# Transpositions of x and B in the chunk stage in the rounded 32-bit type

## The chip, the cores and the metric

The kernel runs on one core of a Trainium2 chip. The core has five engines that work side by side: TensorE (PE in the profile; its weight loads have a row of their own, PEld), VectorE (DVE), ScalarE (ACT), GpSimd (POOL) and SyncE (SP), which here only starts transfers. The metric is device microseconds of one execution; lower is better. Three runs of the kernel before took 1293.86, 1295.33 and 1298.93 us; the median is 1295.33.

## The reference, cut to what matters

One layer of a decoder: a prompt of 1024 rows and 64 sample rows go through a norm, a large projection, two branches (a pooling branch and a state-space branch, "SSD") and a gated sum. The change lies in the state-space branch of the prompt. There the rows are cut into 8 chunks of 128, and the 32 heads stand in 4 groups of 8. For each group and chunk the reference does this:

```python
def step(h, inp):
    xq, dq, Bq, Cq = inp
    acs = jnp.cumsum(dq * Ag, axis=1)
    seg = acs[:, :, None] - acs[:, None, :]
    decay = jnp.exp(jnp.where(mask, seg, -jnp.inf))
    cb = jnp.einsum('bign,bjgn->bijg', Cq, Bq)
    att = cb[..., None] * decay * dq[:, None]
    y = jnp.einsum('bijge,bjgep->bigep', att, xq)
    y = y + jnp.einsum('bign,bige,bgepn->bigep', Cq, jnp.exp(acs), h)
    last = acs[:, -1]
    w_in = jnp.exp(last[:, None] - acs) * dq
    h = h * jnp.exp(last)[..., None, None] + jnp.einsum('bjgn,bjge,bjgep->bgepn', Bq, w_in, xq)
    return h, y
```

`xq` is a chunk of x (512 channels for a group), `Bq` and `Cq` its 128 state columns, and `h` the state that goes from chunk to chunk.

## The kernel before, in words

**Number types.** TensorE takes 32-bit data in two declared types: plain (F32 in the code) and rounded (F32R). For accuracy, the large products are split: a matrix is cut into a rounded part and a rounded rest ("hi" and "lo"), and three products of the rounded type (hi x hi, hi x lo, lo x hi) stand for one. Smaller products are made in the plain type; each of these appears as two pairs of a weight load and a matmul. A transposition is made on TensorE too: the data are loaded as weights and an identity matrix is streamed through, so that the transposed data land in PSUM. There is one identity, `ident`, in the plain type (L112), and all transpositions are in that type. Each is one weight load and one matmul.

**Stages by time.** Up to about 120 us the inputs are normed and transposed and the first products run; the order on every engine is written out by hand there. From 120 to 832 us the projection runs, in Strassen's manner, with convolutions, pooling and the sample part of the state-space branch beside it. From 832 to 1122 us is the chunk stage, which the change touches. Then come the last output products, up to 1297 us.

**The chunk stage.** `chunk(g, c)` (L1382) is a generator for group g and chunk c; there are 4 x 8 = 32. The convolved x, B and C were stored channels-first in DRAM. A chunk loads them as `xb` (six blocks of 128x128: four of x, then B, then C), loads the running sums of the decays into `dec`, copied to all 128 partitions, has ScalarE make `cE` and the eight exponentials of `dec` (L1196) and POOL put in the mask (L1187). Then come the lines that the change touches: four transpositions of x into one PSUM bank `px` (L1400), one of B into another bank `pbc` (L1402), and, in the plain type, the product of B and C beside it (L1403). ScalarE copies the transposed B to a rounded part `bt` (L1406), VectorE makes `xd` from `px` (L1412) and scales `px` in place (L1413); ScalarE and VectorE split it into `xw` and `xwl` (L1415, L1419), and B's rest is `btl` (L1420). VectorE multiplies the decays with the product of B and C (L1416) and `cE` with C (L1418). Next, `inner` (L1203) makes the chunk's output with small plain products (L1208, L1211), three split products make the state's update (L1429 to L1431), and `finish` (L1360) gates and splits the output.

**What sets the order.** The instructions of a chunk are woven with large output products (`products`, L1682, which runs blocks of `gemm_`, L348, with its three split products L354 to L356). TensorE's order in this stage is that of the program text: `in_line` ties each of its instructions to the one before. ScalarE, VectorE, POOL and SyncE are ordered by a planner, which at build time goes through the program with modelled costs and puts on each engine what is ready, by priority; `behind` pins a few pieces. Buffers matter too: `xd`, `bt`, `btl`, `xw` and `xwl` have one buffer each, `dec`, `xb` and `sz` three.

Of the kernel before, what the change touches and what calls it, by code (L numbers as in the profile page):

```python
# [9 lines left out]
F32R = mybir.dt.float32r  # L10
# [10 lines left out]
P = 128  # L21
# [25 lines left out]
def tile_pool_ssd_step(  # L47
# [6 lines left out]
    nc = tc.nc  # L54
    uid = [0]

    def nm(s):
        uid[0] += 1
        return f"{s}_{uid[0]}"
# [33 lines left out]
    def Y4(pool, dt=F32R):  # L93
        return pool.tile([P, 4, T], dt, tag="Y", name=nm("Y"), bufs=2)

    def PB():
        return psB.tile([P, 512], F32, tag="ps", name=nm("ps"))
# [4 lines left out]
    def const(shape, name, dt=F32):  # L102
        return cp.tile(shape, dt, tag=name, name=name)
# [7 lines left out]

    ident = const([P, P], "ident")  # L112
    make_identity(nc, ident)
    blk = const([NS, NB], "blk")
    nc.gpsimd.memset(blk, 1.0)
    nc.gpsimd.affine_select(blk, blk, [[-8, NB]], ALU.is_ge, 0.0, base=0, channel_multiplier=1)
# [1062 lines left out]
    def decays(dec, g, c):  # L1179

        S = P if c < NC else NS
        load(dec, acs_d[c, 8 * g:8 * g + 8, :S].partition_broadcast(S))

    def far(dec, c):

        if c < NC:
            nc.gpsimd.affine_select(dec, dec, [[0, 8], [1, P]], ALU.is_ge, FAR, base=0, channel_multiplier=-1)  # L1187
        else:
            dS = dec.rearrange("p h (b i) -> p h b i", i=8)
            nc.gpsimd.affine_select(dS, dS, [[0, 8], [8, NB], [1, 8]], ALU.is_ge, FAR, base=0, channel_multiplier=-1)  # L1190
            nc.gpsimd.affine_select(dS, dS, [[0, 8], [-8, NB], [0, 8]], ALU.is_ge, FAR, base=0, channel_multiplier=1)

    def exps(dec, g, c):
        S = P if c < NC else NS
        for h in range(8):
            act(dec[:, h], dec[:, h], AF.Exp, bias=acT[:S, c, 8 * g + h:8 * g + h + 1], scale=-1.0)  # L1196
# [6 lines left out]
    def inner(xd, dec, S, state=None, cE=None):  # L1203
        pi = PB()
        for q in range(4):
            o = [pi[64 * hh:64 * hh + 64, q * S:(q + 1) * S] for hh in range(2)]
            for hh in range(2):
                mm(o[hh], xd[:S, 2 * q + hh, :], dec[:S, 2 * q + hh], start=True, stop=state is None)  # L1208
            for hh in range(2 if state is not None else 0):
                h = 2 * q + hh  # L1210
                mm(o[hh], state[:, h * 64:h * 64 + 64], cE[:, h], start=False, stop=True)  # L1211
        return pi[:, :4 * S].rearrange("p (q i) -> p q i", i=S)
# [144 lines left out]
    def ckt(shape, tag, bufs=2):  # L1357
        return (cl if tag in CKL else ca if tag in ("dec", "xb", "cE") else ck).tile(list(shape), F32, tag=tag, name=nm(tag), bufs=bufs)

    def finish(g, o, S, v, sz):  # L1360

        V.tensor_tensor(v, v, sz, ALU.mult)
        act(sz, v, AF.Square)
        nc.gpsimd.tensor_tensor(sz[:, 0:2], sz[:, 0:2], sz[:, 2:4], ALU.add)
        sa = sq_acc[:, o:o + S]
        if g == 0:
            nc.gpsimd.tensor_tensor(sa, sz[:, 0], sz[:, 1], ALU.add)
        else:
            nc.gpsimd.tensor_tensor(sz[:, 0], sz[:, 0], sz[:, 1], ALU.add)
            nc.gpsimd.tensor_tensor(sa, sa, sz[:, 0], ALU.add)  # L1370
        yhc = yh[g][:, :, o:o + S]
        act(yhc, v, AF.Copy)
        nc.gpsimd.tensor_tensor(yl[g][:, :, o:o + S], v, yhc.bitcast(F32), ALU.subtract)
# [8 lines left out]
    def chunk(g, c):  # L1382
        o = c * P
        xb = ckt([P, 6, P], "xb", 3)
        load(xb, xbc_d[g][:, :, o:o + P])
        Bf, Cf = xb[:, 4], xb[:, 5]
        dec = ckt([P, 8, P], "dec", 3)
        decays(dec, g, c)
        yield
        if c > 0:  # L1390
            cE = ckt([P, 8, P], "cE")
            act(cE, dec, AF.Exp, scale=-1.0)
        far(dec, c)
        exps(dec, g, c)
        yield
        sz = ckt([P, 4, P], "sz", 3)
        load(sz, z_d[g][:, :, o:o + P])
        px = PB()
        for q in range(4):
            nc.tensor.transpose(px[:, q * P:(q + 1) * P], xb[:, q], ident)  # L1400
        pbc = PB()
        nc.tensor.transpose(pbc[:, :P], Bf, ident)  # L1402
        mm(pbc[:, P:2 * P], Bf, Cf, start=True, stop=True)  # L1403

        bth, btl = (ck.tile([P, P], F32R, tag=t, name=nm(t), bufs=1) for t in ("bt", "btl"))
        act(bth, pbc[:, :P], AF.Copy)  # L1406
        if c > 0:
            act(pbc[:, 2 * P:3 * P], Cf, AF.Copy)
        pxv = px.rearrange("p (h d) -> p h d", d=64)
        heads = slice(8 * g, 8 * g + 8)  # L1410
        xd = ckt([P, 8, 64], "xd", 1)
        V.tensor_tensor(xd, pxv, dtT[:, c, heads].unsqueeze(2).to_broadcast([P, 8, 64]), ALU.mult)  # L1412
        V.tensor_tensor(pxv, pxv, wdT[:, c, heads].unsqueeze(2).to_broadcast([P, 8, 64]), ALU.mult)  # L1413
        xwh, xwl = (ck.tile([P, 512], F32R, tag=t, name=nm(t), bufs=1) for t in ("xw", "xwl"))
        act(xwh, px, AF.Copy)  # L1415
        V.tensor_tensor(dec, dec, pbc[:, P:2 * P].unsqueeze(1).to_broadcast([P, 8, P]), ALU.mult)  # L1416
        if c > 0:
            V.tensor_tensor(cE, cE, pbc[:, 2 * P:3 * P].unsqueeze(1).to_broadcast([P, 8, P]), ALU.mult)  # L1418
        V.tensor_tensor(xwl, px, xwh.bitcast(F32), ALU.subtract)  # L1419
        V.tensor_tensor(btl, pbc[:, :P], bth.bitcast(F32), ALU.subtract)  # L1420
        xD = ckt([P, 4, P], "xD")
        for q in range(4):
            act(xD[:, q], xb[:, q], AF.Copy, scale=Dv[:, 4 * g + q:4 * g + q + 1])
        yield
        if c == 0:
            yh[g], yl[g] = [Y4(hs if g % 2 else hp) for _ in range(2)]
        pi = inner(xd, dec, P, *((hst[g], cE) if c > 0 else ()))
        pu = PB()
        mm(pu, bth, xwh, start=True, stop=False)  # L1429
        mm(pu, btl, xwh, start=False, stop=False)  # L1430
        mm(pu, bth, xwl, start=False, stop=True)  # L1431
        hn = ckt([P, 512], "hst", 2)
        if c == 0:
            V.tensor_copy(hn, pu)
        else:
            nc.gpsimd.tensor_tensor(hn.rearrange("p (h d) -> p h d", d=64), hst[g].rearrange("p (h d) -> p h d", d=64),
                                    Elb[:, c, heads].unsqueeze(2).to_broadcast([P, 8, 64]), ALU.mult)
            V.tensor_tensor(hn, hn, pu, ALU.add)
        hst[g] = hn

        v = ckt([P, 4, P], "v")
        V.tensor_tensor(v, pi, xD, ALU.add)
        finish(g, o, P, v, sz)
        if c == NC - 1:
            yield
            pt = PB()
            for q in range(4):
                nc.tensor.transpose(pt[:, q * P:(q + 1) * P], hn[:, q * P:(q + 1) * P], ident)
            fo = ckt([P, 4, P], "xD")
            act(fo, pt.rearrange("p (q n) -> p q n", n=P), AF.Copy)  # L1450
            store_(new_ssm_p[0, 0, 8 * g:8 * g + 8].rearrange("(q h) p n -> (h p) q n", h=2), fo)
# [127 lines left out]
    def to_chunks():  # L1579
        nonlocal right, ca  # L1580
        right.__exit__(None, None, None)
        right = tc.tile_pool(name="ca", bufs=3, side="right", reuse_waits="tile")
        ca = right.__enter__()
        right_all.append(right)
        seq.extend(chunk(g, c) for g in range(NG) for c in range(NC))
        next(seq[0])
# [288 lines left out]
    for i in range(8):  # L1875
# [7 lines left out]
        if last_:  # L1883
            q, s3 = hs.tile([P, T], F32, tag="sq", name="q", bufs=1)[:, :D], const([P, 4], "s3")
        rl = sso[:, i:i + 1]
        out = y_prompt[0, i * P:(i + 1) * P, :]
# [59 lines left out]
```

## Time and profile before

| what | value |
|---|---|
| median of three runs | 1295.33 us |
| span of the profiled execution | 1297.1 us |
| its own time | not given beside the span; the span stands for it |
| TensorE busy | 1255.9 us, 97% |
| weight loads busy | 1173.9 us, 90% |
| VectorE / ScalarE / POOL busy | 70% / 55% / 52% |
| chunk stage, 832 to 1122 us | TensorE busy 280.9 of 290 us |

In the lines of the profile, L1400 is line 1400 of the kernel; `ps<-ident,xb` says that the tile `ps` is written from `ident` and `xb`, the moving operand first and then the weights. `128*128 128x128` is the size of the weights and then of the moving operand. A list of a line's instructions gives the shortest, median and longest duration in ns; the timeline gives start and length in us; a row of the waits gives who waited for whom, the sum in us, the number of waits and the longest. Matmuls overlap, and the ends of their records are modelled: what one costs in a row of them is the step from start to start. Both number types stand as `f32` where the shape of a matmul is given.

### The profile page before, as it was taken

To read this page: it belongs to the slowest core of one execution; us is meant where nothing else is said; L and a number is where in the kernel's file an instruction comes from. 1 tells how busy PE (TensorE), PEld (TensorE's weight loads), DVE (VectorE), ACT (ScalarE), POOL (GpSimd) and SP (SyncE) were. 2 spreads that over 40 slices of the span, in tenths; PEclk is the share of its full clock that TensorE was granted. 3 is DMA by queue.
4 is the path that set the end of the run, shared out by engine and by line. 5 is a ranking of instruction groups with operands and counts; after the bars stand their busy time and mean duration, and the time that the engine had idled before them with its cause. 6 is when DMAs were issued, how large, how long until landed. Compare 5 with 4: busy or idle time off the path is not lost.

```text
span 1297.1 us, 26554 instructions
## 1 busy us (share of the span) xinstructions
PE 1255.9 (97%) x9771; PEld 1173.9 (90%) x9771; DVE 910.5 (70%) x1580; ACT 708.8 (55%) x1684; POOL 677.4 (52%) x563
## 2 busy tenths in 40 slices
PE   7999999999999999999999999999998999999998
PEld 6779999989999999999889999889998999999786
DVE  4685778866979578775777665488676888576433
ACT  4665356375656564545455453687987868201111
POOL 1007668677869776664344444276776747314000
PEclk9999999999999999999999999999999999999999
DMA  9837345465455544444656555999988656575631
GB/s 326 259 107 224 119 150 173 142 202 170 146 180 197 165 155 133 161 135 129 181 158 173 152 178 164 356 355 354 338 270 262 202 168 199 172 266 159 226 106 52
DMA packets 233795, 251.70 MB, mean 194 GB/s; under 512 B 31265, under 2 KB 177905, under 8 KB 233658
## 3 DMA queue, kind: packets, MB, share of 16 engines
q1 hardware_dynamic: 161568, 171.60, 42.1%
q10 hardware_dynamic: 72098, 78.41, 17.5%
q8 instruction: 77, 1.26, 0.4%
q14 instruction: 52, 0.43, 0.1%
HBM read 167.06 MB, written 83.01 MB: 193 GB/s over the span
## 4 chain that ended last, share of the span: by engine, by line
PE 67%; issue 8%; DMA 8%; DVE 6%; POOL 5%; ACT 4%; SPq 0%; ACTq 0%; POOLq 0%; DVEq 0%
PE ps L603 6%; PE ps L604 6%; PE ps L605 6%; PE mm L603 6%; PE mm L605 6%; PE mm L604 6%; PE mm L355 3%; PE mm L356 3%; PE mm L354 3%; PE ps L1208 2%; PE ps L1892 2%; PE ps L1894 2%; PE ps L1893 2%; POOL wlo L163 2%; PE ps L1211 2%
## 5 line engine op out<-in xcount | busy, mean ns | idle before, releaser
L163 POOL TENSOR_TENSOR wlo<-rawA,whi 128x512 fp32r<-128x512 f32 x120 | 184.0, 1538 | 185.6 <-ACT whi L160 101.6
L163 POOL TENSOR_TENSOR wlo<-raw,whi 128x512 fp32r<-128x512 f32 x92 | 150.7, 1646 | 125.3 <-ACT whi L160 91.1
L354 PE MATMUL mm<-Y,whi 128*128 128x352 f32 (+1 forms) x480 | 160.1, 334 | 0.7 <-DVE G L1795 0.5
L355 PE MATMUL mm<-Y,whi 128*128 128x352 f32 (+1 forms) x480 | 157.3, 328 | 1.0 <-DVE Y L1466 1.0
L356 PE MATMUL mm<-Y,wlo 128*128 128x352 f32 (+1 forms) x480 | 156.9, 327 | 0.0
L605 PE MATMUL mm<-Y,wlo 128*128 128x272 f32 x496 | 143.6, 290 | 3.9 <-POOL wlo L163 3.1
L603 PE MATMUL ps<-Y,whi 128*128 128x272 f32 x496 | 144.5, 291 | 2.3 <-ACT o L803 1.7
L603 PE MATMUL mm<-Y,whi 128*128 128x272 f32 x496 | 146.5, 295 | 0.2
L604 PE MATMUL ps<-Y,whi 128*128 128x272 f32 x496 | 143.1, 289 | 0.0
L604 PE MATMUL mm<-Y,whi 128*128 128x272 f32 x496 | 142.9, 288 | 0.0
L605 PE MATMUL ps<-Y,wlo 128*128 128x272 f32 x496 | 142.6, 288 | 0.0
L160 ACT ACTIVATE whi<-rawA 128x512 fp32r<-128x512 f32 x125 | 78.2, 626 | 95.6 <-PE ps L604 44.9
L1051 DVE SCALAR_TENSOR_TENSOR GA<-GA,cvT,GA 128x1112 f32<-128x1112 f32 x72 | 127.1, 1769 | 0.6 <-ACT GA L1048 0.5
L160 ACT ACTIVATE whi<-raw 128x512 fp32r<-128x512 f32 x96 | 58.7, 626 | 91.4 <-DVE raw L549 41.7
L605 PEld LDWEIGHTS mm<-Y,wlo 128*128 128x128 f32 x496 | 93.4, 188 | 5.8 <-POOL wlo L163 4.2
L603 PEld LDWEIGHTS ps<-Y,whi 128*128 128x128 f32 x496 | 93.3, 188 | 4.0 <-ACT o L803 1.9
L603 PEld LDWEIGHTS mm<-Y,whi 128*128 128x128 f32 x496 | 93.3, 188 | 2.5 <-issue 0.8
L604 PEld LDWEIGHTS mm<-Y,whi 128*128 128x128 f32 x496 | 93.4, 188 | 0.7 <-issue 0.6
L604 PEld LDWEIGHTS ps<-Y,whi 128*128 128x128 f32 x496 | 93.3, 188 | 0.3 <-issue 0.2
L605 PEld LDWEIGHTS ps<-Y,wlo 128*128 128x128 f32 x496 | 93.4, 188 | 0.2 <-issue 0.2
L354 PEld LDWEIGHTS mm<-Y,whi 128*128 128x128 f32 x480 | 90.3, 188 | 3.2 <-DVE G L1795 1.4
L355 PEld LDWEIGHTS mm<-Y,whi 128*128 128x128 f32 x480 | 90.3, 188 | 3.2 <-DVE Y L1466 1.6
(452 smaller groups left out, 3851.6 us busy)
## 6 DMA issues: line engine op xcount, KB each, us to landing
rawA<-in_w_in SPq DMA_DIRECT2D x46, 512.0 KB
dec<-acs_d SPq DMA_DIRECT2D x32, 512.0 KB
xbc<-GA ACTq DMA_DIRECT2D x24, 512.0 KB
xb<-xbc SPq DMA_DIRECT2D x32, 384.0 KB
rawA<-in_w_in SPq DMA_DIRECT2D x32, 256.0 KB
pw<-in_w_ssm_out ACTq DMA_DIRECT2D x32, 256.0 KB
ws<-ph ACTq DMA_DIRECT2D x32, 256.0 KB
ws<-pw SPq DMA_DIRECT2D x32, 256.0 KB
```

Of the source, the lines that this page charges most:

```text
L160: ins = act(hi[:, :, :ncols], raw[:, :, :ncols], AF.Copy)
L163: (eng or nc.gpsimd).tensor_tensor(lo[:, :, :ncols], raw[:, :, :ncols], hi[:, :, :ncols].bitcast(F32), ALU.subtract)
L354: mm(ps[:, :n], a, rh[k][:, o:o + n], start=(k == 0), stop=False)
L355: mm(ps[:, :n], a, rl[k][:, o:o + n], start=False, stop=False)
L356: mm(ps[:, :n], b, rh[k][:, o:o + n], start=False, stop=(k == nk - 1))
L603: mm(p, hi, ah, start=(k == 0), stop=False)
L604: mm(p, hi, al, start=False, stop=False)
L605: mm(p, lo, ah, start=False, stop=(k == 3))
L1051: V.scalar_tensor_tensor(d[:, :n], rp[:, k:k + n], cvT[:, 24 * k + mc:24 * k + mc + 1], d[:, :n], ALU.mult, ALU.add)
L1208: mm(o[hh], xd[:S, 2 * q + hh, :], dec[:S, 2 * q + hh], start=True, stop=state is None)
L1211: mm(o[hh], state[:, h * 64:h * 64 + 64], cE[:, h], start=False, stop=True)
L1892: mm(ps[:, :cw], mhk, wo[k][0][:, s], start=(k == 0), stop=False)
```

## The change

A second identity in the rounded type, `identR`, is made at the start by a copy on POOL. A helper, `turnR`, declares the output, the data and the identity of a transposition in the rounded type. The four transpositions of x and the one of B in each chunk use it; all other transpositions keep `ident`. The identity takes 512 more bytes per partition of SBUF, and the program is made with a scratch area for DMA of 1024 bytes per partition; before, it was 16384 by default.

```diff
@@ -111,6 +111,12 @@
 
     ident = const([P, P], "ident")
     make_identity(nc, ident)
+    identR = const([P, P], "identR", F32R)
+    nc.gpsimd.tensor_copy(identR, ident)
+
+    def turnR(out, src):
+        nc.tensor.transpose(out.bitcast(F32R), src.bitcast(F32R), identR)
+
     blk = const([NS, NB], "blk")
@@ -1397,9 +1403,9 @@
         load(sz, z_d[g][:, :, o:o + P])
         px = PB()
         for q in range(4):
-            nc.tensor.transpose(px[:, q * P:(q + 1) * P], xb[:, q], ident)
+            turnR(px[:, q * P:(q + 1) * P], xb[:, q])
         pbc = PB()
-        nc.tensor.transpose(pbc[:, :P], Bf, ident)
+        turnR(pbc[:, :P], Bf)
         mm(pbc[:, P:2 * P], Bf, Cf, start=True, stop=True)
@@ -1930,7 +1936,7 @@
-    nc = _bacc.Bacc("TRN2", target_bir_lowering=False, num_devices=1)
+    nc = _bacc.Bacc("TRN2", target_bir_lowering=False, num_devices=1, dynamic_dma_scratch_size=1024)
```

## The prediction

> **What bounds the kernel now.** I read the page first, then the table of windows by stage, then the waits of TensorE in the chunk stage, then the instructions one by one around one group of transpositions.
>
> ```profile
> span 1297.1 us, 26554 instructions
> PE 1255.9 (97%) x9771; PEld 1173.9 (90%) x9771; DVE 910.5 (70%) x1580; ACT 708.8 (55%) x1684; POOL 677.4 (52%) x563
> PE 67%; issue 8%; DMA 8%; DVE 6%; POOL 5%; ACT 4%; SPq 0%; ACTq 0%; POOLq 0%; DVEq 0%
> ```
>
> TensorE is busy for 97% of the span, and it carries most of the chain that ended last. All that shortens TensorE's own stream is worth its full length, as long as the stage has no other limit close behind. The changed lines run in the chunk stage, from 832 to 1122 us:
>
> ```profile
> 832.00:1122.00 290.00, 280.90 (x2306) 260.51 (x2305) 228.02 (x348) 224.44 (x612) 185.38 (x210) 1.00 0.80 257
> ```
>
> The columns are length, then busy time of PE, PEld, DVE, ACT, POOL, the granted clock, DMA share and GB/s. TensorE idles 290.0 - 280.9 = 9.1 us here; per chunk (32 of them, 9.06 us each) DVE has 7.1 us of work and ACT 7.0 us, so both could follow a chunk some 2 us shorter. The clock is 1.00. One chunk's group, PE first, then PEld (start us, length us):
>
> ```profile
> 933.29 0.32 PE L355 MATMUL mm<-Y,whi 128*128 128x352 f32 x1
> 933.46 0.33 PE L356 MATMUL mm<-Y,wlo 128*128 128x352 f32 x1
> 933.62 0.60 PE L1400 MATMUL ps<-ident,xb 128*128 128x128 f32 x4
> 934.05 0.27 PE L1402 MATMUL ps<-ident,xb 128*128 128x128 f32 x1
> 934.16 0.39 PE L1403 MATMUL ps<-xb 128*128 128x128 f32 x2
> 934.30 0.42 PE L354 MATMUL mm<-Y,whi 128*128 128x384 f32 x1
> 934.56 0.34 PE L355 MATMUL mm<-Y,whi 128*128 128x384 f32 x1
> ```
>
> ```profile
> 933.46 0.52 PEld L1400 LDWEIGHTS ps<-ident,xb 128*128 128x128 f32 x4
> 933.95 0.14 PEld L1402 LDWEIGHTS ps<-ident,xb 128*128 128x128 f32 x1
> 934.05 0.30 PEld L1403 LDWEIGHTS ps<-xb 128*128 128x128 f32 x2
> 934.28 0.19 PEld L354 LDWEIGHTS mm<-Y,whi 128*128 128x128 f32 x1
> 934.39 0.19 PEld L355 LDWEIGHTS mm<-Y,whi 128*128 128x128 f32 x1
> ```
>
> The record of a matmul is long (0.27 us) but overlaps the next; what it costs is the step from start to start. From 933.62 to 934.16 five transpositions start: 0.54 us, 108 to 109 ns each. There is no hole before or behind them: the product ahead and the product behind keep their step. So the group is 0.54 us of TensorE time per chunk, 32 x 0.54 = 17.4 us in the stage, all of it on the path.
>
> **What limits a transposition to 109 ns.** A transposition has two halves that overlap its neighbours': the load of the data as weights, and the stream of 128 columns of the identity. The records of loads of other widths tell them apart:
>
> ```profile
> L1289 PE MATMUL ps<-ident,h x128: 270/272/328, 614.5 to 797.0; 128*128 128x128 f32 x128
> L1400 PEld LDWEIGHTS ps<-ident,xb x128: 138/140/143, 832.7 to 1102.1; 128*128 128x128 f32 x128
> L1400 PE MATMUL ps<-ident,xb x128: 270/272/273, 832.8 to 1102.2; 128*128 128x128 f32 x128
> L1061 PEld LDWEIGHTS ps<-ident,t x24: 103/103/105, 178.7 to 547.3; 128*27 128x27 f32 x24
> L1239 PEld LDWEIGHTS ps<-ident,hst x16: 108/110/112, 598.8 to 757.8; 128*64 128x64 f32 x16
> ```
>
> ```profile
> L1403 PEld LDWEIGHTS ps<-xb x64: 190/191/192, 833.3 to 1102.5; 128*128 128x128 f32 x64
> L1241 PEld LDWEIGHTS ps<-hst x8: 132/134/136, 599.8 to 758.2; 128*64 128x64 f32 x8
> ```
>
> A plain load goes from 134 ns at 64 columns to 191 at 128, 0.89 ns per column, some 110 ns for 128; the first two loads behind the group, which are in the rounded type, also step by 934.39 - 934.28 = 0.11 us. A transposition's load goes from 110 to 140 ns, 0.47 per column, some 55 to 60 ns for 128. The idle case agrees: the longest L1289 record, 328 ns, is 56 above its median, one load that nothing hid. So the load, at about 56 ns, is not what makes 109; the stream is: 128 columns at 0.85 ns. The plain 32-bit products stream at the same rate, and the rounded type at half of it:
>
> ```profile
> L809 PE MATMUL ps<-GA,pwt x24: 379/486/539, 167.5 to 474.4; 128*128 128x256 f32 x8, 128*128 128x384 f32 x8, 128*128 128x448 f32 x8
> ```
>
> ```profile
> 1284.80 0.28 PE L1892 MATMUL ps<-Y,m 128*128 128x256 f32 x1
> ...
> 1286.21 0.28 PE L1892 MATMUL ps<-m,G 128*128 128x256 f32 x1
> ```
>
> L809 (32-bit) gains 160 ns from 256 to 448 columns, 0.83 ns per column. L1892 to L1894 (rounded type) have 12 products between the two rows, 1.41 / 12 = 0.1175 us for 256 columns, 0.46 ns per column with all that comes with one; 352 columns took 160 ns (933.46 to 933.62), so each of the 96 columns between costs 0.44 ns.
>
> **The change, part by part.** (a) The stream of the 160 transpositions. If the rounded type streams the identity once per column, as it does for every product in it, 128 columns cost 117.5 - 128 x 0.44 = 61 to 62 ns, with the load of 56 ns still hidden behind the stream. The lower end for the step is the load itself, 56 ns. The upper end, for rows of the plain type, is the present 109, or worse where the load becomes plain (rivals). I take 62, from the nearest row in the same type, the 256-column one. Not all five gain. The fifth (L1402) is followed by L1403, a plain 32-bit product whose load of 110 ns starts when the fifth starts; so L1403 still starts 110 ns behind it. Four steps per chunk shrink by 109 - 62 = 47 ns: 0.188 us, over 32 chunks 6.0 us. With a step of 56 it is 4 x 53 x 32 = 6.8 us.
>
> (b) What of it reaches the end. TensorE's order in this stage is written out by hand, so all behind the group moves forward. Its waits there are short and rare:
>
> ```profile
> PE ps L1208 <- DVE dec L1416: 3.4, 3, 1.4
> PEld ps L1208 <- DVE dec L1416: 4.8, 5, 1.7
> ```
>
> These hang on L1403 and on ScalarE's exponentials; the first moves forward by the same 0.188 us, and the second has 2 us of slack per chunk on average. I count the full 6.0 us. The sum of the DMA shares, 0.80, leaves a fifth free for a stage 2% shorter.
>
> (c) The readers of the transposed data (L1406, L1412) get it 0.2 us sooner, worth nothing by itself: VectorE's L1412 waits for another thing, the release of its output tile by the products of the previous chunk:
>
> ```profile
> DVE xd L1412 <- PE ps L1208: 35.2, 27, 3.8
> ```
>
> (d) The second identity: one POOL copy of 128x128 at the start. Copies on POOL:
>
> ```profile
> L1257 POOL COPY yt<-hst 128x480 f32<-128x480 f32 x8 | 5.4, 680 | 8.4 <-DVE xd L1321 6.5 <-DMA hst<-xbc 1.9
> L1150 POOL COPY sel<-ident 64x96 f32<-64x96 f32 x2 | 0.5, 264 | 0.0
> ```
>
> Between them, 0.30 us for 128 columns. POOL's setup ends with the memset of the sums, and the first to read those waits for a transfer:
>
> ```profile
> 2.55 0.10 POOL L185 MEMSET ss<- 128x9 f32 x1
> 5.00 1.23 DVE L201 SCALAR_TENSOR_TENSOR sqj<-Y 128x1024 f32<-128x1024 f32 x1 [5.00 <-DMA Y<-in_x_prompt]
> ```
>
> From 2.65 to 5.00 us is 2.35 us of cover for 0.30, so the copy costs nothing; without that cover it would cost 0.3 us once. Its 512 bytes per partition only move addresses.
>
> (e) The smaller DMA scratch. All data transfers go by these two queues:
>
> ```profile
> q1 hardware_dynamic: 161568, 171.60, 42.1%
> q10 hardware_dynamic: 72098, 78.41, 17.5%
> ```
>
> All of them are issued by SyncE and ScalarE, none by POOL, and the two instruction queues beside them fetch code. Nothing in the trace shows a use of the scratch, so I take nothing, to either side; a use would show as issues or landings that take another time than now.
>
> The sum: -6.0 us. The profiled execution spans 1297.1 us, 1.8 above the median of the runs, 1295.33, and within them (1293.86 to 1298.93); it goes to 1291.1, and the median to 1289.3. That is 0.46%. What a measurement of this kernel can tell from no change is about 0.5%, 6.5 us, so a correct sum may still read as no change.
>
> **The rivals.**
>
> 1. *No change, 1295.3.* The transposition mode streams at its own rate, whatever the declared type, or the load of the rounded type is a plain one (110 ns) and takes the place of the stream as the limit: either gives a step of 108 to 112 ns, within 0.5 us of now. For it: no transposition in the rounded type is in this trace, and its plain loads are as slow as those of the 32-bit type. Against it: all rows have the stream's rate set by the type, and the short load goes with the transposition, not with the type. The Trainium skill, in "TensorE: Matmul & The Clock Gate", section "Terms", says that the transposition mode makes 32-bit data four times faster; were that so, the 32-bit transposition would already stream once per column and there would be nothing to gain, 1295.3. The trace does not agree: a 32-bit product has two records (24 for L809's 12 products) of 0.83 ns per column, 1.66 in all; a transposition has one record of 0.85, so it is twice as fast and not four times.
>
> 2. *Slower by the order of the other engines.* Only TensorE's order is written out in this stage; that of ScalarE, VectorE, POOL and the transfers comes from a planner that weighs modelled costs, and a transposition in another type has another cost there. If a swap puts work ahead of L1196's exponentials or of VectorE's L1416, TensorE stands at L1208 for it. The rows in (b) give the price: 8.2 us in 8 waits, 1 us each. The gain of 6.0 us is eaten by 6 such waits, and slower by more than 6.5 us takes 13 of the 32 chunks: 1302, and 1307 with 18. For it: VectorE and ScalarE are each 77 to 79% busy here. Against it: the change in cost is small, 0.2 us against the 2 us that each has over per chunk. The same swap can also go well, by at most the 9.1 us of idle time.
>
> 3. *Slower by the stream.* A rounded stream as narrow as 128 columns is in no row; the narrowest is 256. Should it take two passes with plain loads, the step is 2 x 110 = 220 ns, and 160 x 111 ns = 17.8 us is lost: 1313. It decides from 150 ns up (160 x 41 ns = 6.5 us). Against it: from 512 to 256 columns nothing of the kind begins.
>
> **How the numbers follow.** Gain as summed, 0.50, with 1286.5 to 1291.5 as its own range (6.8 us with a step of 56 ns, 6.0 with 62, and 2 us of order or of measurement to either side); no change, 0.25; the planner's order against it, 0.13; the narrow stream, 0.06; a better order beside the gain, 0.06, 1283. The likeliest is 1289.3. The range, 1283 to 1302, takes in the better order, no change, and the mild end of rival 2. Faster by over 0.5% means under 1288.85: nearly half of the first case (0.24), the last case (0.06) and a little of no change by chance (0.02): 0.32. Slower means over 1301.8: most of rivals 2 and 3 and a tail of no change, 0.20. The rest is 0.48.
>
> **What would show it.** In the group, the starts of L1400's four matmuls step by about 62 ns instead of 109 and the record falls from 272 ns to some 215; L1402 to L1403 stays at 0.11 us; the loads stay at 140 ns. Steps of 109 mean rival 1, and if the load then reads 190 ns, its second form. Steps over 150 mean rival 3. The window of the stage is 5 to 6 us shorter with about 9 us of idle time on TensorE; a shorter busy time with more idle time, at L1208 above all, means rival 2. The POOL copy ends before 3 us and nothing waits for it. The prediction is wrong if the stage's work moves by more than its transpositions, or if stages before 832 us change: nothing in the argument touches these.

## The result, and the profile after

The changed kernel takes 1306.01 us (median of 20 runs, 1301.78 to 1311.03) against 1297.62 for the kernel before on the same chip (20 runs, 1293.86 to 1304.47). The ratio is 1.006, with a 95% interval of 1.0048 to 1.0072: slower by 8.4 us, where the prediction had 6.0 us of gain.

The page of the profile after, its span, the busy time by engine, TensorE's granted clock in 40 slices, and the shares of the chain:

```profile
span 1304.7 us, 26560 instructions
PE 1259.7 (97%) x9771; PEld 1176.9 (90%) x9771; DVE 903.8 (69%) x1580; ACT 709.4 (54%) x1684; POOL 680.9 (52%) x564
PEclk9999999999999999999999999989999999999999
PE 74%; DMA 9%; DVE 6%; issue 4%; ACT 3%; POOL 2%; ACTq 0%; SPq 0%; POOLq 0%; DVEq 0%
```

The span is 7.6 us longer than before's 1297.1, and TensorE's busy time grew by 3.8 us, though 160 of its instructions were meant to shrink. The 8 in the clock row is slice 27, from 848 to 881 us, inside the chunk stage. The window of that stage (columns as in the prediction):

```profile
832.00:1122.00 290.00, 275.49 (x2248) 254.22 (x2246) 223.70 (x343) 227.37 (x619) 178.79 (x201) 0.98 0.79 257
```

TensorE idles 14.5 us in it, against 9.1 before, and the clock is 0.98. In the same 290 us only 2248 matmuls are done, not 2306.

**The transpositions did get faster.** One group in the timeline of the kernel after, PE first, then PEld (L118 is the line in `turnR`; the other lines moved down by six):

```profile
919.10 0.34 PE L362 MATMUL mm<-Y,wlo 128*128 128x384 f32 x1
919.28 0.54 PE L118 MATMUL ps<-identR,xb 128*128 128x128 f32 x5
919.66 0.46 PE L1409 MATMUL ps<-xb 128*128 128x128 f32 x2
919.87 0.41 PE L360 MATMUL mm<-Y,whi 128*128 128x352 f32 x1
```

```profile
919.10 0.57 PEld L118 LDWEIGHTS ps<-identR,xb 128*128 128x128 f32 x5
919.62 0.30 PEld L1409 LDWEIGHTS ps<-xb 128*128 128x128 f32 x2
919.84 0.19 PEld L360 LDWEIGHTS mm<-Y,whi 128*128 128x128 f32 x1
```

From the first transposition's start to that of L1409, 919.28 to 919.66, it is 0.38 us instead of 0.54. But L1409 then needs 0.21 us to the next product instead of 0.14 (934.16 to 934.30 before), since its first weight load starts only at 919.62. From the first transposition to the product behind the group it is 0.59 us; before it was 934.30 - 933.62 = 0.68. That is 0.09 us per group. The steps of the weight loads, from the second transposition's to that of L1409, say the same: 83, 88, 83 and 87 ns here against 108, 109, 109 and 110. Over all 32 groups the time from the first transposition to the product behind sums to 19.0 us, against 22.1 before: 3.1 us, half of what the prediction counted (the expectations below have it as 32 x 0.094 = 3.0 us). The steps between the five starts are 58, 62, 89 and 83 ns: the first two as predicted, the next two not.

**Where the time went: two long waits.** TensorE runs the same order in both kernels, so the start of each matmul can be compared with the start of the same one before. The difference is 2.1 us at 832 us, 6.4 at 842, 11.8 at 860, 12.8 at 978, 8.3 from 1000 to 1109, and 7.6 at the end (us, places by the time before; between 978 and 1000 the kernel before has waits of 2.0 and 0.9 us that the kernel after does not have). The waits between 830 and 876 us, of the kernel after (engine, place, what it waited for: us in total, times, longest):

```profile
PEld ps L1214 <- DVE dec L1422: 10.2, 2, 5.8
PE ps L1214 <- DVE dec L1422: 9.6, 2, 5.5
...
DVE dec L1422 <- ACT bt L1412: 6.3, 1, 6.3
...
DVE dec L1422 <- ACT dec L1202: 3.6, 1, 3.6
```

and of the kernel before:

```profile
PEld ps L1208 <- DVE dec L1416: 3.1, 2, 1.7
...
PE ps L1208 <- DVE dec L1416: 2.5, 2, 1.4
```

The same two waits, at the first small product that reads the decays, grew from 2.5 to 9.6 us. VectorE could not multiply the decays (L1422) because ScalarE's work came late: by the rows above, its first wait ended with the copy `bt` (L1412), which stands on ScalarE behind the exponentials of two chunks (L1202), and its second with exponentials. ScalarE's timeline, kernel after:

```profile
826.56 0.43 ACT L721 ACTIVATE u<-u 128x272 f32<-128x272 f32 x1 [4.83 <-DMA xb<-xbc]
826.90 0.61 ACT L1680 ACTIVATE ph<-pw 128x512 fp32r<-128x512 f32 x1
...
829.51 0.33 ACTq L1681 DMA_DIRECT2D wo<-ph  x1
830.27 0.33 ACTq L723 DMA_DIRECT2D gs<-u  x1
830.63 1.28 ACT L1202 ACT_TABLE_LOAD   x1 [2.80 <-DMA wlo<-wp]
831.92 2.45 ACT L1202 ACTIVATE dec<-dec,acT 128x128 f32<-128x128 f32 x8
...
840.38 0.40 ACT L1202 ACTIVATE dec<-dec,acT 128x128 f32<-128x128 f32 x1 [1.20 <-POOL dec L1193]
840.68 2.13 ACT L1202 ACTIVATE dec<-dec,acT 128x128 f32<-128x128 f32 x7
842.73 0.25 ACT L1412 ACTIVATE bt<-ps 128x128 fp32r<-128x128 f32 x1
```

and before:

```profile
821.66 0.75 ACT L715 ACTIVATE u<-u 128x272 f32<-128x272 f32 x2 [2.17 <-DMA wlo<-wp]
...
822.81 1.28 ACT L1196 ACT_TABLE_LOAD   x1 [0.39 <-ACT u L715]
824.10 2.45 ACT L1196 ACTIVATE dec<-dec,acT 128x128 f32<-128x128 f32 x8
...
832.90 2.14 ACT L1196 ACTIVATE dec<-dec,acT 128x128 f32<-128x128 f32 x7
834.95 0.25 ACT L1406 ACTIVATE bt<-ps 128x128 fp32r<-128x128 f32 x1
```

Both chunks' exponentials, and the copy behind them, are 7.8 us later. The rows add it up: ScalarE came to this place 2.2 us later; its idle time is 4.83 + 2.80 us instead of 2.17 + 0.39, which is 5.1 more; and the copy of an early split (L1680) adds 0.5. The idle time ends with stores in ScalarE's own queue (the rows ACTq), which wait for transfers. The early split's store (L1681) is one of them, but the last to go is the projection's own (L723, 830.27), so how much of the 5.1 us is due to the early loads is not settled by these rows. TensorE's first wait, 4.1 us, ends behind the copy at 842.73; the second, 5.5 us up to 867.5, ends behind the first eight of 16 exponentials that ScalarE runs in one piece from 863.68 on, behind other work. What changed ahead of all this is seen in SyncE's queue. Rows of the output weights' splits (`wo_splits`) and of the gates' loads, after:

```profile
802.43 0.34 SPq L1674 DMA_DIRECT2D pw<-in_w_o  x1
812.44 0.68 SPq L1674 DMA_DIRECT2D pw<-in_w_o  x1
...
824.91 0.36 SPq L1676 DMA_DIRECT2D wo<-pw  x1
...
831.85 0.32 SPq L1676 DMA_DIRECT2D wo<-pw  x1
...
846.73 2.66 SPq L1403 DMA_DIRECT2D sz<-z  x3
```

and before:

```profile
831.64 3.31 SPq L1397 DMA_DIRECT2D sz<-z  x3
839.93 0.42 SPq L1668 DMA_DIRECT2D pw<-in_w_o  x1
841.79 0.97 SPq L1668 DMA_DIRECT2D pw<-in_w_o  x1
849.18 0.32 SPq L1670 DMA_DIRECT2D wo<-pw  x1
```

The loads for the late splits start 37 us earlier. Their copies on ScalarE (L1680), their subtractions on POOL (L1682) and their stores in SyncE's queue now stand among the first chunks' own preparation. Why they can start earlier is seen in the memory plan that the build makes. In the kernel before, the first buffer `pw` of these loads (bytes 187,712 to 189,760 of a partition) overlaps the buffers `c2` of the projection (187,360 to 189,536); the last store of the `c` tiles was issued at 815.5 us:

```profile
L717 ACTq DMA_DIRECT2D gs<-c x3: 340/347/349, 764.6 to 815.5; - x3
```

With the smaller scratch `pw` lies at the same place, but no `c2` does any more, so these tiles no longer hold the load back. Why the planner, in the kernel before, left the load for another 24 us behind that store stays open, so the overlap shows what kept the load from 802 us, not what put it at 840.

**And the clock behind each wait.** The window view at the two waits (length, busy PE, PEld, DVE, ACT, POOL, granted clock, DMA share, GB/s):

```profile
840.96:844.37 3.41, 0.01 (x2) 0.01 (x2) 1.29 (x2) 2.50 (x9) 0.00 (x0) 1.00 0.96 349
844.37:847.78 3.41, 3.41 (x20) 2.80 (x21) 3.29 (x7) 0.00 (x0) 0.00 (x0) 0.51 0.48 164
...
861.44:864.85 3.41, 0.55 (x4) 0.26 (x2) 0.53 (x1) 3.41 (x12) 3.41 (x5) 1.00 1.04 409
864.85:868.26 3.41, 0.69 (x4) 0.29 (x4) 2.06 (x2) 3.41 (x13) 1.20 (x2) 0.51 0.75 244
868.26:871.68 3.42, 2.99 (x28) 2.89 (x28) 0.60 (x3) 0.70 (x2) 1.26 (x1) 0.50 0.66 239
```

After a stretch of 3.41 us with little or no work, the next 3.41 us are granted half the clock, though TensorE is busy again; the last row follows a stretch that was slow and mostly idle itself. At that clock the small products of L1214 and L1217 step by 0.43 us per four (869.14 to 871.28 us), against 0.22 at full clock (939.11 to 940.20). So half of the busy time is lost, (3.41 + 0.69 + 2.99) / 2 = 3.5 us here, an estimate. So the account in the profile is: the entry to the stage +2.1; the two waits 9.6 - 2.5 = +7.1; the half-speed stretches behind them +3.5; the transpositions -3.1; the two waits of before at 978 to 1000 that are gone -2.9. The sum is +6.7; the trace shows +7.6. The other waits of the stage, 4.5 us against 3.6 before, make up the rest. The +2.1 at the entry cannot be put down to the order: the two versions in the old order, shown below, enter the stage 2.4 and 1.9 us late in their profiles, and the changed kernel, profiled a second time, 0.5 us late.

### The profile page after: what moved, and what is told of

Its sections match the earlier page's. It is cut to its first block, busy times and chain, and to the rows that moved or that the text cites. A ratio compares the mean times of both kernels' runs of the same rounds, so it can differ in the third digit from the quotient of the medians.

```text
span 1304.7 us, 26560 instructions
## 1 busy us (share of the span) xinstructions
PE 1259.7 (97%) x9771; PEld 1176.9 (90%) x9771; DVE 903.8 (69%) x1580; ACT 709.4 (54%) x1684; POOL 680.9 (52%) x564
## 4 chain that ended last, share of the span: by engine, by line
PE 74%; DMA 9%; DVE 6%; issue 4%; ACT 3%; POOL 2%; ACTq 0%; SPq 0%; POOLq 0%; DVEq 0%
PE ps L609 7%; PE ps L610 7%; PE ps L611 7%; PE mm L609 7%; PE mm L611 6%; PE mm L610 6%; PE mm L360 4%; PE mm L362 4%; PE mm L361 4%; PE ps L1898 2%; PE ps L1900 2%; PE ps L1899 2%; PE ps L1214 2%; PE ps L234 2%; PE ps L1217 2%
```

## The experiments

Two theories were left after this profile. In the first, A, the transpositions give 3 us and the new order of the other engines, which comes from the planner, costs more than that; in its narrower form the room that the smaller scratch frees makes that order. In the rival, B, the order is harmless and the rounded transpositions themselves cost the time, by the clock for one. The first four kernels were measured together, against 35 runs of the kernel before with a median of 1300.87 us.

**The type alone, in the old order.** The smaller scratch is left out; 15,872 is a size at which all else keeps its place when the second identity is added. ScalarE, VectorE, POOL and SyncE are tied to the order they had before:

```diff
-    nc = _bacc.Bacc("TRN2", target_bir_lowering=False, num_devices=1, dynamic_dma_scratch_size=1024)
+    nc = _bacc.Bacc("TRN2", target_bir_lowering=False, num_devices=1, dynamic_dma_scratch_size=15872)
...
+    for engine, names in _ORDER.items():
+        for a, b in zip(names, names[1:]):
+            tc.add_manual_dep(by[f"I-{b}"], f"I-{a}", mybir.DependencyInfo(
+                mybir.DependencyClass.NoSync, mybir.DependencyReason.DATA), reason="order")
```

> The change's transpositions in the rounded type, with ScalarE, VectorE, POOL and the transfer queues tied to the order that they have in the kernel before (the scratch is 15872 bytes, just small enough for the second identity). Theory A (the order of the other engines costs the time, the transpositions themselves gain): the group of a chunk keeps steps of about 58, 62, 86, 84 and 86 ns, worth 32 x 0.094 = 3.0 us, the two stalls of 4 and 5 us before L1208 are gone, and the time is 2 to 3 us under the kernel before, ratio 0.998. Theory B (the rounded transpositions themselves cost, by way of the clock, which fell to half in three windows of the chunk stage): the half-clock windows stay and the time is 5 to 9 us over the kernel before, ratio 1.004 to 1.007.

Measured: 1298.40 us, ratio 0.9979 (0.9962 to 0.9997). By the ratio that is 2.7 us of gain (0.4 to 4.9), with the 3.0 us of the step arithmetic inside, and none of the loss. The waits between 830 and 876 us are those of before:

```profile
PE ps L1214 <- DVE dec L1422: 2.5, 2, 1.4
```

The rounded transpositions do not cost the time.

**Plain transpositions in the new order.** The mirror image: `turnR`'s two calls go back to `nc.tensor.transpose(..., ident)`, the second identity is made but not used, the scratch stays small, and the four engines are tied to the order of the changed kernel.

```diff
-            turnR(px[:, q * P:(q + 1) * P], xb[:, q])
+            nc.tensor.transpose(px[:, q * P:(q + 1) * P], xb[:, q], ident)
...
-        turnR(pbc[:, :P], Bf)
+        nc.tensor.transpose(pbc[:, :P], Bf, ident)
```

> All transpositions in the plain type as before, with the scratch of 1024 bytes, the second identity made but not used, and the other engines tied to the order that they have in the changed kernel. Theory A: both stalls before L1208 in the first chunks are there, and the 3.0 us of the transpositions are not gained: 9 to 12 us over the kernel before, ratio 1.007 to 1.009. Theory B: as the kernel before, ratio 1.000, clock 1.00 through the chunk stage.

Measured: 1306.69 us, ratio 1.0041 (1.0025 to 1.0057), in the profile with waits of 4.2 and 5.4 us at the same two places and half-speed stretches behind both. The loss comes with the order, without a single rounded transposition. Its size fell short of the expectation; a later run comes back to that.

**The smaller scratch alone.** The kernel before with one argument added:

```diff
-    nc = _bacc.Bacc("TRN2", target_bir_lowering=False, num_devices=1)
+    nc = _bacc.Bacc("TRN2", target_bir_lowering=False, num_devices=1, dynamic_dma_scratch_size=1024)
```

> The kernel before with the smaller DMA scratch alone; no second identity, all transpositions plain; nothing is tied. Theory A1 (14.8 KB more room per partition let the planner start the splitting of the output weights some 37 us earlier, and these loads got ahead of the chunks'): the first two loads of pw stand at about 802 and 812 us as in the changed kernel, L1208 stalls by several us in the first chunks, ratio 1.004 to 1.009. Theory A2 (the order moved by the modelled cost of the transpositions, the scratch does nothing): pw first near 840 us, ratio 1.000.

Measured: 1308.11 us, ratio 1.0050 (1.0032 to 1.0068). One argument, which no instruction in the traces is seen to use, gives a loss as large as that of the whole change. The early load and the two waits are there (SyncE's timeline, and the waits from 830 to 876 us):

```profile
802.49 0.34 SPq L1668 DMA_DIRECT2D pw<-in_w_o  x1
```

```profile
PE ps L1208 <- DVE dec L1416: 9.5, 2, 5.4
```

**The type alone, planner free.** The changed kernel with a scratch of 15,872:

```diff
-    nc = _bacc.Bacc("TRN2", target_bir_lowering=False, num_devices=1, dynamic_dma_scratch_size=1024)
+    nc = _bacc.Bacc("TRN2", target_bir_lowering=False, num_devices=1, dynamic_dma_scratch_size=15872)
```

> The rounded transpositions with a scratch of 15872 bytes, so without the extra room; nothing is tied. Theory A1: the pw loads stay near 840 us and the large stalls are absent; what the planner moves for the type's modelled cost costs or gains at most 2 us, and the 3.0 us of the transpositions show: ratio 0.996 to 1.000. Theory A2: the two stalls are there and the ratio is that of the change, 1.006.

Measured: 1304.12 us, ratio 1.0013 (0.9996 to 1.0030), above what was expected. The late loads stay late (845.3 us), but the planner makes another order for the new type as well, with one wait of 3.0 us at 839 us. This kernel lies 0.0034 above the same one in the old order, so the planner's order for the type and the second identity eats the type's gain. Each part of the change, alone, moved the order to the worse.

The next four ran together on another chip, against 17 runs of the kernel before with a median of 1299.16 us.

**Both parts in the old order.** As the first experiment, but with the scratch of 1,024 bytes, so that addresses and scratch are those of the change.

> Both parts of the change, with ScalarE, VectorE, POOL and SyncE tied to the order they had before. Theory A (only the order costs time; the smaller scratch and the moved addresses cost nothing): as the type alone in the old order, 0.998, within 0.996 to 1.000, with waits of 1 to 2 us at the product that reads the decays. Theory B (the smaller scratch costs time by itself, by addresses or by slower transfers): 1.002 to 1.006.

Measured: 1299.05 us, ratio 0.9995 (0.9977 to 1.0013). This is inside the range of A and below that of B; the same two parts with the planner's order gave 1.0051 beside it, so the order is worth 0.0056, some 7 us. Whether the scratch and the addresses cost a small rest is not settled: 0.9995 lies 0.0016 above the first experiment, with intervals that overlap.

**The early loads held back.** The whole change with the planner free, except that the first two loads of the late splits must stand behind an earlier transfer of the chunks:

```diff
             if n < 16:
                 raws[n] = ck.tile([P, 512], F32, tag="pw", name=nm("pw"), bufs=2)
-                load(raws[n], w_o[0, n // 2 * P:n // 2 * P + P, n % 2 * 512:n % 2 * 512 + 512])
+                with behind(mybir.EngineType.SP, 14) if n < 2 else ExitStack():
+                    load(raws[n], w_o[0, n // 2 * P:n // 2 * P + P, n % 2 * 512:n % 2 * 512 + 512])
```

> The whole change, planner free, but the first two loads of the output weights for the late splits may not start before the transfers of the chunk before them. Theory A1 (those two loads, started 37 us early, are the cause: their splits and stores stand ahead of the chunk stage's own loads): no wait above 2 us between 832 and 876 us, ratio 0.996 to 1.000. Theory A2 (any new order is worse than the old one; the early loads are only its first sign): waits of 3 us or more somewhere in the chunk stage, ratio 1.002 to 1.007.

Measured: 1313.30 us, ratio 1.0107 (1.0087 to 1.0128), the slowest of all. This tie moves the loads much further than the old place (SyncE's timeline), and the waits from 832 to 1122 us are many and short:

```profile
910.39 0.42 SPq L1675 DMA_DIRECT2D pw<-in_w_o  x1
```

```profile
PEld ps L1214 <- DVE dec L1422: 12.9, 9, 2.4
PE ps L1214 <- DVE dec L1422: 10.2, 9, 2.1
...
PE ps L1217 <- DVE cE L1424: 6.7, 9, 0.8
```

The two long waits at 840 and 862 us are gone (by 875 us this kernel is 2.4 us behind before, the changed one 11.5), which, with the run of the smaller scratch alone, points to the early loads as their cause; the planner made the rest of the order anew here too, so they are not isolated. But the splits, pushed to 910 us, then crowd the middle of the stage: between 900 and 1040 us the kernel falls 13 us further behind. The narrow theory holds for its place and fails for the total: the order of before was a good one among worse, on either side of it.

**The changed kernel again, and plain transpositions in its order again.**

> The changed kernel once more, beside the others on one chip: 1.006 by its first measurement, within 1.004 to 1.008.

> Plain transpositions in the order of the changed kernel, once more, beside the changed kernel itself. If the 3 us of the faster transpositions are worth the same in either order: 0.0023 above the changed kernel, 1.008. If the new order's long waits swallow them (what TensorE saves ahead of a wait, it spends in it): as the changed kernel, 1.005 to 1.007.

Measured: 1306.07 us, 1.0051 (1.0033 to 1.0068), and 1306.99 us, 1.0056 (1.0038 to 1.0074). The two are 0.9 us apart in the expected direction, but less than the 3.0 us of the groups. The profiles show one reason: the changed kernel had two half-speed stretches behind its first wait in this run (842.2 to 849.0 us), the plain one had one. From 875 to 1122 us the two profiled executions of the changed kernel come 3.2 and 5.0 us closer to the kernel before, the two plain ones 2.5 and 2.4. With intervals this wide, whether the gain is kept or partly swallowed in the new order stays open.

**What sets the step.** In the kernel with the type alone and the old order for the other engines (in this build some of TensorE's products of the sample stage stand elsewhere), the x transpositions of the sample stage are made rounded too:

```diff
-            nc.tensor.transpose(px[:S, q * P:(q + 1) * P], xb[:, q], ident)
+            turnR(px[:S, q * P:(q + 1) * P], xb[:, q])
```

> Both kinds of rounded transposition side by side: the chunk stage's with loads of 128 columns and, new, those of x in the sample stage with loads of 64 columns; both stream 128 columns of the identity. If the load sets the step of 83 to 89 ns in the chunk stage, the sample stage's steps fall from 109 ns to about 60 ns and stay there for all steps of a group. If the stream sets it, they are 83 to 89 ns there too.

A single run (1301.41 us beside one run of before at 1300.81) tells nothing of the total. The timeline at one group of the sample stage, and the records of both widths:

```profile
599.96 0.41 PE L118 MATMUL ps<-identR,hst 128*64 128x128 f32 x4
600.21 0.34 PE L609 MATMUL mm<-Y,whi 128*128 128x272 f32 x1
```

```profile
L118 PEld LDWEIGHTS ps<-identR,xb x160: 137/140/146, 834.5 to 1103.0; 128*128 128x128 f32 x160
...
L118 PEld LDWEIGHTS ps<-identR,hst x16: 108/109/112, 599.8 to 759.8; 128*64 128x64 f32 x16
```

Four transpositions take 0.25 us, 58 to 64 ns each in all four groups, and the weight loads step by 59 to 63 ns from the second on. With 128 columns to load and the same 128 to stream, the chunk stage's steps in the same run are 80 to 90 ns from the third on (one group with a wait inside left out). So the stream needs at most some 60 ns, and the load sets the rest. In the kernel before, plain, the same four groups of the sample stage step by 108 to 110 ns, as the chunk stage does: there the stream is the limit with either load.

## Why the prediction was wrong, point by point

**(a) The step of a transposition: the stream right, the load mis-sized, the gain half.** The stream's 61 to 62 ns was right, by the first two steps and by the sample stage. The term that was mis-sized is the load: I took it as 55 to 60 ns from the difference of two records, hidden behind the stream, and it steps at 82 to 91 ns, so that the load, not the stream, is the limit from the third transposition of a group on. The difference of records of two widths left some 25 to 30 ns of the step out (86 ns in the median). The late load also reached L1409, which I had expected to start 110 ns behind the fifth transposition and to keep its own step; its step to the next grew by 70 ns. The term is 3.1 us, not 6.0. The Trainium skill, in "TensorE: Matmul & The Clock Gate", section "Back-to-back issue gap", gives about 81 ns for a sustained pair of load and matmul with 128 columns; the 80 to 89 ns between these starts, from the third on, come near it. By that figure the term would have been 4 x 28 x 32 = 3.6 us, an estimate.

**(b) That the gain reaches the end: not in the kernel that was built.** With the order held, the type alone kept 2.7 us of 3.0 (0.9979), both parts together 0.6 us (0.9995), with intervals that leave room for all of it or little. The waits between 830 and 876 us were as short as I said in the old order; in the kernel that was built they were not.

**(c) and (d) held.** The readers' earlier data changed nothing that was seen. The copy of the identity took 0.285 us against 0.30, starting at 1.8 us:

```profile
L115 POOL CAST identR<-ident x1: 285/285/285, 1.8 to 1.8; 128x128 fp32r<-128x128 f32 x1
```

**(e) The scratch: the step that failed.** I looked for instructions that use the scratch, found none, and took nothing to either side. Whether it costs anything by itself is not settled by the old order (0.9995 against 0.9979). But the scratch is room in the same memory as the tiles, and the planner orders work by when a buffer is free. The argument "only move addresses" was made for the identity's 512 bytes; moving addresses is what changes which tile waits for which. The Trainium skill, in "SBUF — State Buffer", section "SBUF size: 192, 224, or 256?", puts the scratch at 16 KiB of each partition; no run here shows that figure itself, but it is the hint that some 15 KiB came free, an estimate by that page.

**The rivals.** Rival 2, slower by the order of the other engines, is what happened, and at the place it named, the product that waits for the decays. I gave it 0.13, on the ground that the transposition's cost in the plan changes little. The ground was wrong in two ways: the cause was the scratch, which I had not connected with the planner, and a planner's answer need not be small when its input is (the type alone gave a 3.0-us wait). Its price was wrong too: I counted 13 waits of 1 us; two of 4 and 5.5 us were enough, and each was followed by half-speed stretches, which stood nowhere in my sum. The 8.2 us in 8 waits also counted the same waits twice, for most of them stand in PE's row and in PEld's; TensorE's own were 3.4 us in 3. The form I described, many short waits, is the one of the held loads: nine waits, 10.2 us. Rivals 1 and 3 fell, for the step is neither 109 ns nor above 150; but rival 1's second form was right that the load takes the stream's place as the limit, at 82 to 91 ns instead of 110.

**What would show it.** The text said that a shorter busy time with more idle time at that product means rival 2; the idle time rose by 5.4 us in the stage's window, and half of the sign was missing, since half-speed stretches lengthen busy time. It also said that the prediction is wrong if stages before 832 us change: the loads at 802 us are such a change.

## What to carry to other kernels

Where a planner or an allocator sets the order, a change of memory (a freed scratch, one more tile) is a change of schedule: list which buffers overlap before and after and what each held back, and price it by the waits at the stage's tightest product, not by the bytes. To learn what an edit is worth by itself, hold the order of the engines that it does not touch, as the first experiment did; that version, at 0.9979, is also the only one measured clear of the kernel before on the fast side, by little (the interval ends at 0.9997). And size a chain of loads by the step between two of their starts, from rows of the same width, not by the slope of their records alone.

## What was not expected of the hardware

**Half speed comes in fixed slots of 3.41 us.** In the ten traces with half-speed stretches before the end, all of these begin and end on a grid of 3.413 us that runs through the whole execution, with another offset in each. Of 40 half-speed slots, 36 follow a slot in which TensorE was idle for 47% or more of the time; the other four follow slots with 0, 0, 17 and 27% of idle time, the last two of these half-speed themselves, and they are not explained. Behind the first 16 us, no slot with more than 54% of idle time was followed by full speed; between 47 and 54% both happened. So what a wait of 2 to 3 us costs depends on where it falls in the grid: the wait of 2.4 us at 664 us left the clock at 1.00 in the kernel before, and a wait of 2.2 us there was followed by 0.50 in the kernel after, at the same place in the program. In the run of the type alone with the planner free, the wait of 3.0 us at 839 us lay across two slots, idle for some 40 and 50%, and the clock stayed full. The waits of 4 us and more, ten in the chunk stages of five traces, were all followed by half speed. The median granted clock of the runs agrees with the traces: 0.992 for the changed kernel, 0.996 for the kernel before beside the first four experiments, 0.996 for both versions in the old order. The Trainium skill, in "TensorE: Matmul & The Clock Gate", section "What's actually happening", describes a free-running window of 3413 ns; the traces agree with that. Its table under "Why this matters for your kernels" sets the limit at idle gaps of about 3 us, one window; here a window half idle was enough, and the measurement decides.

**A rounded transposition of 128 columns is limited by its load,** 80 to 90 ns from the third on. In the plain type it is 108 to 110 ns with a load of 128 or of 64 columns, so the stream limits it there; in the rounded type with a load of 64 columns it is 58 to 64 ns.
